# Stick-breaking attention in a hybrid decoder step: page tiles and weight tiles with places of their own

## The chip, the core and the metric

The kernel runs on one NeuronCore of a Trainium2 chip. The metric is the device time of one execution in microseconds (us), as the median of several runs. A profile records one further execution: what each engine did and when. The engines are PE (TensorE, matmuls and transposes), DVE (VectorE), ACT (ScalarE), POOL (GpSimd, which also issues the indirect DMAs) and SP (which issues the other DMAs).

## The reference

One layer of a decoder step for a prompt of 512 tokens behind 16 meta tokens, and for 8 running sequences of 4 new tokens each. All of it is float32.

```python
h = x + 0.5 * rms_norm(swiglu(rms_norm(x, ...), ...), ...)
u = rms_norm(h, mix_pre_g)
proj = u @ w_in          # q, k, v of GLA and of the stick-breaking branch, gates
o_a  = gla_branch(...)   # gated linear attention
o_b  = sb_attend(q_b, keys, vals, sb_bias, q_off)
m = sigmoid(gate_a) * (o_a @ w_o_gla) + sigmoid(gate_b) * (o_b @ w_o_sb)
h = h + rms_norm(m @ w_out, mix_post_g)
y = h + 0.5 * rms_norm(swiglu(rms_norm(h, ...), ...), ...)
```

The change lies in the stick-breaking attention, which has 16 heads of 64. For a query t and the keys s before it:

```python
z = q @ k / sqrt(64) + bias
A[t, s] = sigmoid(z[t, s]) * prod_{s < j < t} (1 - sigmoid(z[t, j]))
o[t] = sum_s A[t, s] * v[s]
```

The prompt attends to itself (528 tokens). Each running sequence attends to 256 cached tokens as well, which lie in 2 pages of 128 tokens of a paged cache (`cache_k`, `cache_v`, found through `page_table`).

## The kernel before

All tokens (512 of the prompt, 32 new ones, 16 meta) lie side by side in the free dimension; features lie in the partitions. A large product is made in three float32r matmuls per tile: `hi` weights with the `hi` and the `lo` part of the activations (L232, L233), `lo` weights with the `hi` part (L235). One **step** of a product is one of its 8 slices of 128 features, for both halves of the tokens: six matmuls. Weights come by DMA into `raw`, ACT copies them to `hi` (L192), DVE subtracts to `lo` (L139, the line of the helper `tt`, which makes all two-operand work).

Almost all other tiles are cut from one arena by `take(width)` and given back by `give(...)`. A tile that is taken again must wait until everything that read or wrote its last tenant is done. Which place is used is decided when the program is built, from the order of the calls.

The stage that is changed is a loop `for pr in range(9)` over 8 pairs of heads; I call one turn of it a **pass**. In pass `pr` PE makes the query, key and value products of pair `now` (24 steps), and between the steps, at places that are written out by hand (`in_q`, `in_k`, `in_v`: after step 1 to 8 of each product), it does the following.

- For the pair before (`last`): `rows_v` and `rows_k` transpose the new rows and write them to DRAM (L895, L884); `rows_v` also splits the values into `hi` and `lo` (`vsp`, the `lo` on POOL); `tails` transposes the last rows and a zero-padded copy of the meta values (`vfm`, filled by two POOL copies, L912). `turned(e, n)` transposes a part of the weights of head `e` (L933) and splits them into `ah` (ACT, L936) and `al` (DVE, L139); `summed(e, n)` multiplies them with the values (L948 to L950, of which the second reads `al`). `meta_turned` and `meta_summed` do the meta part, ending with a copy on ACT (L967).
- For `now`, `scores(e)` after value step 3 (head 0) and 5 (head 1): products on PE (L854, L855) into three banks; two sigmoids of each on ACT (L858, L859) into `keep` and `beta`; 8 triangular selects on POOL (L863); 5 scans on DVE (L867) and three products with `beta` (L139); then four POOL copies of the meta columns into `am` (L876).
- In passes 5 to 8, the samples: `sample_keys` transposes the four gathered pages (16 transposes, L1034, at query steps 1, 3, 5, 7) and `sample_products` multiplies them with the new queries (L1047).

A page is fetched by an indirect DMA on POOL (L992) into a tile from `take(512)`:

```python
if pr > 4:
    kp, kT = pages_of(ck, 0, pr - 5), {}     # four gathers, ahead of the queries
```

PE's order in this loop is fixed by hand. The order on the other engines, and on PE elsewhere, is made by a scheduler when the program is built; on the chip each engine works through its own list in order.

After the loop, `sample_weights` turns the sums of the samples into attention weights (L1070, L1087), and a stage of 8 gate products follows in which `sample_values` (L1154, needs value pages) and `sample_scores` for the second half of the heads (needs key pages) alternate; a stage of 16 products with four more `sample_values` comes next.

Of the kernel before, what the change touches and what calls it, by code (L numbers as in the profile page):

```python
# [9 lines left out]
F32R = mybir.dt.float32r  # L10
# [97 lines left out]
def hybrid_step(  # L108
# [647 lines left out]
        G.memset(t, 0.0)  # L756


    klz = [[take(nk, F32R) for _ in range(2)] for _ in range(2)]
    for t in (*klz[0], *klz[1]):  # L760
        G.memset(t.bitcast(F32), 0.0)

    def qzp(pr, more=128):
# [16 lines left out]
    def steps(main, at):  # L780

        n = 0
        while True:
# [5 lines left out]
            for f in at.get(n, ()):  # L789
                f()  # L790

    class Pair:


        def __init__(self, pr):
            self.pr, self.c0 = pr, P * pr
            self.betas = []

        def queries(self, at):
            pr = self.pr  # L800
# [17 lines left out]
        def keys(self, at):  # L818
            pr = self.pr
            acc = steps(gemm_steps(win, C_KB + self.c0, P, KD, um, (0, 1), HW), at)  # L820

            self.kf = kf = take(NT)
            S.copy(kf[:, NTL : NTL + HW], acc[0][:, :HW])
            S.copy(kf[:, NTL + HW :], acc[1][:, : NP - HW])
            S.copy(kf[:, :NTL], acc[1][:, NP - HW : HW])
            self.ks = ks = [take(nk, F32R) for _ in range(2)]
            self.kl = kl = klz[pr % 2]
            for e in range(2):
                src = kf[own_[e], NS:]
                V.tensor_copy(ks[e][own_[e]], src)  # L830
                S.copy(ks[e][other[e]], src)
                tt(kl[e][own_[e]], src, ks[e][own_[e]].bitcast(F32), ALU.subtract)
            V.tensor_copy(kns[:, NS * pr : NS * pr + NS], kf[:, :NS])

        def values(self, at):
            acc = steps(gemm_steps(win, C_VB + self.c0, P, KD, um, (0, 1), HW), at)
            self.vf = vf = take(NT)
            for h in range(2):
                S.copy(vf[:, h * HW : h * HW + HW], acc[h][:, :HW])

        def scores(self, e):
            hh = 2 * self.pr + e
            qs, ks, kl = self.qs, self.ks, self.kl
            if e == 0:
                self.am = take(P)

            beta, keep = (take(832), take(NP)), (take(832), take(NP))
            for n, what in enumerate(BANKS):
                p = ps()
                c = 0  # L850
                for i, k0, k1 in what:
                    qc, kc = slice(P * i, P * i + P), slice(k0, k1)
                    o = p[:, c : c + k1 - k0]
                    T.matmul(o, qs[e][:, qc], ks[e][:, kc], start=True, stop=False)  # L854
                    T.matmul(o, qs[e][:, qc], kl[e][:, kc], start=False, stop=True)  # L855
                    c += k1 - k0
                d = slice(416 * (n % 2), 416 * (n % 2) + c)
                S.activation(keep[n // 2][:, d], p[:, :c], AF.Sigmoid, bias=sbb[:, 16 + hh : 17 + hh], scale=-1.0)  # L858
                S.activation(beta[n // 2][:, d], p[:, :c], AF.Sigmoid, bias=sbb[:, hh : hh + 1])  # L859
            for i, a, b in PARTS:  # L860
                for t, fill in ((keep, 1.0), (beta, 0.0)):
                    d = t[i // 3][:, b - P : b]
                    G.affine_select(out=d, in_=d, pattern=[[-1, P]], compare_op=ALU.is_ge, fill=fill, base=-1,  # L863
                                    channel_multiplier=1)
            for i, a, b in PARTS + ((2, 816, 832),):
                k = keep[i // 3][:, a:b][:, ::-1]
                V.tensor_tensor_scan(out=k, data0=k, data1=k, initial=keep[1][:, :1] if a == 816 else 1.0,  # L867
                                     op0=ALU.mult, op1=ALU.bypass)
            for d, k in ((beta[0][:, :831], keep[0][:, 1:832]), (beta[0][:, 831:832], keep[1][:, :1]),
                         (beta[1][:, : NP - 1], keep[1][:, 1:])):  # L870
                tt(d, d, k, ALU.mult)
            give(*keep)
            self.betas.append(beta)
            for i in range(4):
                a = (0, 144, 416, 816)[i]
                G.tensor_copy(self.am[:, 2 * NM * i + NM * e : 2 * NM * i + NM * e + NM], beta[0][:, a : a + NM])  # L876
            if e:
                give(*qs, *ks)

# [26 lines left out]

        def tails(self):
            pr, kf, vf = self.pr, self.kf, self.vf
            vz = vfm[pr % 2]
            for e in range(2):  # L910
                o = vz[own_[e]].rearrange("p (i e k) -> p i e k", e=2, k=NM)[:, :, e]
                G.tensor_copy(o, vf[own_[e], NP + NS :].unsqueeze(1).to_broadcast([64, 4, NM]))  # L912
            p = ps()
            T.transpose(p[:NTL, :P], kf[:, :NTL], ident)
            T.transpose(p[:NTL, P : 2 * P], vf[:, NP:], ident)
            T.transpose(p[:, 2 * P : 3 * P], vz, ident)
            fc = slice(P * (pr % 4), P * (pr % 4) + P)
            self.vm = vm = take(P)
            V.tensor_copy(tail_k[pr // 4][:NTL, fc], p[:NTL, :P])
            V.tensor_copy(tail_v[pr // 4][:NTL, fc], p[:NTL, P : 2 * P])  # L920
            V.tensor_copy(vm, p[:, 2 * P : 3 * P])
            give(kf, vf)
# [17 lines left out]
        def summed(self, e, n):  # L940

            where, ah, al = self.at.pop((e, n))
            if (e, n) == (0, 0):
                self.op = ps()
            for j, c in where:
                o, w = self.op[:, P * j :], P * (4 - j)
                vh, vl = (t[:, P * j : P * j + P] for t in vsp[e])
                T.matmul(o, vh, ah[:, c : c + w], start=(j == 0 and e == 0), stop=False)  # L948
                T.matmul(o, vh, al[:, c : c + w], start=False, stop=False)  # L949
                T.matmul(o, vl, ah[:, c : c + w], start=False, stop=False)  # L950
            give(ah, al)
            if n == len(TILES) - 1:
                give(*self.betas[e])

        at = property(lambda self: self.__dict__.setdefault("at_", {}))

# [30 lines left out]
    ck = cache_k.rearrange("o n s (c h) d -> (o n s c) (h d)", c=2)  # L987
    cv = cache_v.rearrange("o n s (c h) d -> (o n s c) (h d)", c=2)

    def page(src, i, c):  # L990
        t = take(512)
        G.indirect_dma_start(out=t, out_offset=None, in_=src,  # L992
                             in_offset=bass.IndirectOffsetOnAxis(ap=idx[c][:, i : i + 1].bitcast(U32), axis=0))
        return t
# [30 lines left out]
    def pages_of(src, c, b0):  # L1025
        return {(b, pg): page(src, 2 * b + pg, c) for b in (b0, b0 + 4) for pg in range(2)}

    def sample_keys(b, q, kp, kT):

        p = ps()  # L1030
        for r in range(2):
            f = slice(P * (2 * q + r), P * (2 * q + r) + P)
            for pg in range(2):
                T.transpose(p[:, 256 * r + P * pg : 256 * r + P * pg + P], kp[b, pg][:, f], ident)  # L1034
        kT[b, q] = take(512)
        (S.copy if q else V.tensor_copy)(kT[b, q], p)
        if q:
            give(kp[b, 0], kp[b, 1])

    def sample_products(c, b0, kT, z):  # L1040

# [60 lines left out]

    z = take(512)
    with tc.manual_schedule(engines={mybir.EngineType.PE}):
        last = None
        for pr in range(9):
            now = Pair(pr) if pr < 8 else None
            in_q, in_k, in_v = {}, {}, {}
            if last:
# [8 lines left out]
                in_v[4] = [lambda: last.turned(1, 2), lambda: last.summed(1, 1)]  # L1118
                in_v[6] = [lambda: last.summed(1, 2), last.meta_summed]
            if pr > 4:  # L1120
                kp, kT = pages_of(ck, 0, pr - 5), {}
                for n, (b, q) in enumerate((b, q) for b in (pr - 5, pr - 1) for q in range(2)):
                    in_q.setdefault(2 * n + 1, []).append(lambda b=b, q=q: sample_keys(b, q, kp, kT))
                in_k[1] = [lambda: sample_products(0, pr - 5, kT, z)]
            if now:
                in_v.setdefault(3, []).append(lambda: now.scores(0))
                in_v.setdefault(5, []).append(lambda: now.scores(1))
                now.queries(in_q)
                now.keys(in_k)
                now.values(in_v)  # L1130
            else:
# [2 lines left out]
                        for f in at[n]:  # L1134
                            f()
            last = now
    give(*vfm, *klz[0], *klz[1], *vsp[0], *vsp[1], mmask)
    sample_weights(0, z)
    give(z)
    for c in range(2):  # L1140
# [6 lines left out]
    def sample_values(c, b0, vp, oz):  # L1147

        for pg in range(2):
            for i in range(4):  # L1150
                q, r = 2 * c + i // 2, i % 2
                for b in (b0, b0 + 4):
                    row = slice(64 * r + 32 * (b // 4), 64 * r + 32 * (b // 4) + 32)
                    T.matmul(oz[row, P * q : P * q + P], aT[q, pg][:, 256 * r + 32 * b : 256 * r + 32 * b + 32],  # L1154
                             vp[b, pg][:, P * i : P * i + P], start=False, stop=(b0 == 3 and c == 1 and pg == 1 and i > 1))
        give(*vp.values())
        if b0 == 3:
            give(*(aT[g, pg] for g in (2 * c, 2 * c + 1) for pg in range(2)))

# [22 lines left out]

    oas, oap = Parts(), []
    z, oz = take(512), ps()
    vp = pages_of(cv, 0, 0)
    kp = pages_of(ck, 1, 0)
    sample_new(0, oz)
# [22 lines left out]
    for n in range(8):  # L1210
        if n % 2 == 0:
            sample_values(1, n // 2, vp, oz)
            vp = pages_of(cv, 1, n // 2 + 1) if n < 6 else {}
        acc = mgemm(C_GA + P * n, P, W1)
        sg = take(NW)
        for h in range(2):
# [97 lines left out]
```

## Time and profile before

| | us |
|---|---|
| median of 3 runs | 1711.05 (1708.38 to 1714.02) |
| profiled execution | 1711.21 |
| its span, first to last instruction | 1709.5 |
| PE busy | 1615.0 (94%) |
| DVE busy | 805.1 (47%) |
| ACT busy | 637.3 (37%) |
| POOL busy | 340.4 (20%) |
| mean granted clock of PE | 0.982 |

The page gives the busy time of each engine over the whole span. A windows view gives, for stretches that one chooses, the length, the busy time of PE, of its weight loads (PEld), of DVE, ACT and POOL with the number of instructions, the granted clock of PE, the DMAs' busy share and GB/s. A view of waits gives the waiting engine with its line, what ended the wait, the total in us, how often, and the longest. A timeline gives start, duration, engine, line and operation, and in brackets the idle time of the engine just before and what ended it. Line numbers are those of the kernel before.

### The profile page before, as it was taken

The page shows a single profiled execution, that of the slowest core. Times are in us where ns is not written, and L with a number is a line of the kernel's source. Part 1 is how long each engine was busy: PE and PEld are TensorE (multiplying, and loading weights), DVE is VectorE, ACT ScalarE, POOL GpSimd, SP SyncE. Part 2 cuts the span into 40 slices and gives each one's busy share as a digit, 9 for nine tenths or more (in the row PEclk, how much of TensorE's full clock was granted, in tenths as well). Part 3 has the DMA queues.
Part 4 walks back from the last instruction along what each step waited for, and adds up shares of the span by engine and source line. Part 5 has one row for each costly group of instructions (what it writes and reads, how often), then busy time and mean ns, then how long its engine had stood idle before and what let it go on. Part 6 is the DMA issues. An engine that isn't in the chain of part 4 may idle for free.

```text
span 1709.5 us, 29997 instructions
## 1 busy us (share of the span) xinstructions
PE 1615.0 (94%) x12473; PEld 1548.1 (91%) x12473; DVE 805.1 (47%) x1371; ACT 637.3 (37%) x1094; POOL 340.4 (20%) x480
## 2 busy tenths in 40 slices
PE   7999999999798999998787999999999999999997
PEld 6999999999687788888776798999999999999997
DVE  5533333326545676776554543243545333332246
ACT  6422222224334345565443332233346322222233
POOL 2111111100110124244333762010301111110001
PEclk9999999999899999999998999999999999999998
DMA  6422222234666444424333566344403323233243
GB/s 167 136 87 87 87 87 83 80 91 136 142 121 131 124 94 76 78 57 92 78 63 71 174 168 184 82 76 128 136 26 99 112 87 87 87 87 90 83 128 114
DMA packets 296776, 176.02 MB, mean 103 GB/s; under 512 B 9002, under 2 KB 288640, under 8 KB 296640
## 3 DMA queue, kind: packets, MB, share of 16 engines
q1 hardware_dynamic: 291200, 157.25, 37.1%
q0 software_dynamic: 5440, 16.85, 2.8%
q8 instruction: 98, 1.61, 0.4%
q14 instruction: 38, 0.31, 0.1%
HBM read 160.25 MB, written 13.83 MB: 102 GB/s over the span
## 4 chain that ended last, share of the span: by engine, by line
PE 54%; DVE 6%; DMA 6%; issue 5%; ACT 2%; POOL 1%; SPq 0%; ACTq 0%; POOLq 0%; DVEq 0%
PE acc L232 15%; PE acc L233 15%; PE acc L235 15%; DMA raw<-in_w_in_dram 4%; DVE room L139 2%; DVE room L142 1%; DVE lo L139 1%; DMA room<-in_cache_k_dram,idx 1%; ACT hi L192 1%; PE ps L1034 1%; DMA out_dram<-room 1%; DVE room L867 1%; PE ps L949 1%; PE ps L933 1%; POOL room L863 1%
## 5 line engine op out<-in xcount | busy, mean ns | idle before, releaser
L232 PE MATMUL acc<-room,hi 128*128 128x280 f32 (+2 forms) x3440 | 969.3, 295 | 4.2 <-ACT hi L192 3.5
L233 PE MATMUL acc<-room,hi 128*128 128x280 f32 (+2 forms) x3440 | 952.9, 292 | 0.0
L235 PE MATMUL acc<-room,lo 128*128 128x280 f32 (+2 forms) x3440 | 774.9, 292 | 3.0 <-DVE lo L139 2.9
L232 PEld LDWEIGHTS acc<-room,hi 128*128 128x128 f32 (+1 forms) x3440 | 651.6, 189 | 17.0 <-issue 7.5
L233 PEld LDWEIGHTS acc<-room,hi 128*128 128x128 f32 (+1 forms) x3440 | 651.8, 190 | 8.5 <-issue 5.8
L235 PEld LDWEIGHTS acc<-room,lo 128*128 128x128 f32 (+1 forms) x3440 | 562.0, 189 | 6.7 <-DVE lo L139 4.1
L192 ACT CAST hi<-raw 128x1024 fp32r<-128x1024 f32 (+1 forms) x258 | 264.5, 1025 | 743.3 <-PE acc L233 639.7
L139 DVE TENSOR_TENSOR lo<-raw,hi 128x1024 fp32r<-128x1024 f32 (+1 forms) x258 | 312.6, 1212 | 306.8 <-ACT hi L192 300.3
L139 POOL TENSOR_TENSOR room<-room,room 128x544 fp32r<-128x544 f32 (+6 forms) x118 | 148.7, 1270 | 988.5 <-ACT room L394 471.7
L139 DVE TENSOR_TENSOR room<-acc,room 128x280 f32<-128x280 f32 (+1 forms) x262 | 106.6, 440 | 395.0 <-PE acc L235 394.4
L139 DVE TENSOR_TENSOR room<-room,room 128x280 f32<-128x280 f32 (+10 forms) x173 | 98.1, 583 | 31.5 <-ACT room L260 24.9
L863 POOL TENSOR_SCALAR_AFFINE_SELECT room<-room 128x128 f32<-128x128 f32 x128 | 56.1, 463 | 96.5 <-ACT room L858 93.4
L867 DVE TENSOR_TENSOR_SCAN room<-room 128x144 f32<-128x144 f32 (+4 forms) x71 | 58.4, 846 | 17.5 <-POOL room L863 16.1
L139 DVE TENSOR_TENSOR room<-ps,room 128x384 fp32r<-128x384 f32 (+3 forms) x64 | 35.9, 577 | 20.0 <-ACT room L936 19.5
L992 POOL DMA_INDIRECT room<-in_cache_v_dram,idx x32 | 35.7, 1114 | 32.7 <-DMA out_dram<-room 8.4
L992 POOL DMA_INDIRECT room<-in_cache_k_dram,idx x32 | 33.1, 1034 | 42.0 <-PE ps L959 16.1
L854 PE MATMUL ps<-room,room 128*128 128x144 f32 (+4 forms) x75 | 23.2, 327 | 16.9 <-DVE room L139 14.5
L858 ACT ACTIVATE room<-ps,sbb 128x416 f32<-128x416 f32 (+1 forms) x48 | 30.5, 640 | 21.6 <-PE ps L855 18.4
L936 ACT CAST room<-ps 128x384 fp32r<-128x384 f32 (+1 forms) x48 | 24.5, 515 | 28.6 <-PE ps L933 28.5
L260 ACT ACTIVATE room<-room 128x280 f32<-128x280 f32 (+1 forms) x56 | 24.1, 432 | 29.0 <-DVE room L139 22.6
L1034 PE MATMUL ps<-ident,room 128*128 128x128 f32 x128 | 18.9, 283 | 15.1 <-DMA room<-in_cache_k_dram,idx 15.1
L394 ACT CAST room<-room 128x560 fp32r<-128x560 f32 (+1 forms) x44 | 28.8, 655 | 11.6 <-DVE room L139 9.9
(302 smaller groups left out, 1249.7 us busy)
## 6 DMA issues: line engine op xcount, KB each, us to landing
raw<-in_w_in_dram SPq DMA_DIRECT2D x72, 512.0 KB, 8.8
raw<-in_ffn_w_gate_dram SPq DMA_DIRECT2D x50, 512.0 KB, 3.8
raw<-in_ffn_w_up_dram SPq DMA_DIRECT2D x50, 512.0 KB, 3.9
raw<-in_ffn_w_down_dram SPq DMA_DIRECT2D x44, 448.0 KB, 3.7
raw<-in_ffn_w_down_dram SPq DMA_DIRECT2D x22, 512.0 KB, 3.9
out_dram<-room SPq DMA_DIRECT2D x40, 256.0 KB, 3.4
room<-in_state_gla_dram SPq DMA_DIRECT2D x16, 256.0 KB, 3.8
raw<-in_w_o_gla_dram SPq DMA_DIRECT2D x8, 512.0 KB, 4.5
```

Source lines behind the costliest of these rows:

```text
L139: (eng or V).tensor_tensor(out=out, in0=a, in1=b, op=op)
L192: S.copy(hi, raw)
L232: T.matmul(o, wh, a[h][0], start=(k == 0), stop=False)
L233: T.matmul(o, wh, a[h][1], start=False, stop=False)
L235: T.matmul(acc[h][:nw, : wid[h]], wl, a[h][0], start=False, stop=(k == kt - 1))
L394: S.copy(hi[:, c], sl[:, c])
L858: S.activation(keep[n // 2][:, d], p[:, :c], AF.Sigmoid, bias=sbb[:, 16 + hh : 17 + hh], scale=-1.0)
L863: G.affine_select(out=d, in_=d, pattern=[[-1, P]], compare_op=ALU.is_ge, fill=fill, base=-1, channel_multiplier=1)
L867: V.tensor_tensor_scan(out=k, data0=k, data1=k, initial=keep[1][:, :1] if a == 816 else 1.0, op0=ALU.mult, op1=ALU.bypass)
L936: S.copy(ah[:, :c], p[:, :c])
L992: G.indirect_dma_start(out=t, out_offset=None, in_=src, in_offset=bass.IndirectOffsetOnAxis(ap=idx[c][:, i : i + 1].bitcast(U32), axis=0))
L1034: T.transpose(p[:, 256 * r + P * pg : 256 * r + P * pg + P], kp[b, pg][:, f], ident)
```

## The change

It has these parts.

1. `wide`: four sets of tiles (832 and 512 wide) are taken once for `beta` and `keep` and used in turn, in place of `take` and `give` in every call of `scores`. The sets of both `keep` come back at the end of `scores(1)`, those of `beta` when `summed` of the next pass has read them. For that, `scores(1)` moves from value step 5 to 6, behind `summed(1, 2)` and `meta_summed`.
2. `ring`: page tiles are taken once (four from pass 4, four more after the loop) and used in turn. The gathers for the next pass are written down after the queries of this one, from pass 4 on. After the loop, key and value pages share the ring of eight.
3. The four `am` copies of a head move from POOL to DVE. The two `vfm` copies move to DVE as well, and from `tails` to the end of `values`, one pass part earlier.
4. `klz`, the zero-padded `lo` parts of the keys, is one set in place of two in turn.

```diff
-    klz = [[take(nk, F32R) for _ in range(2)] for _ in range(2)]
-    for t in (*klz[0], *klz[1]):
+    klz = [take(nk, F32R) for _ in range(2)]
+    for t in klz:
...
+    wide = [(take(832), take(NP)) for _ in range(4)]
...
-            self.kl = kl = klz[pr % 2]
+            self.kl = kl = klz
...
         def values(self, at):
...
+            vz = vfm[self.pr % 2]
+            for e in range(2):
+                o = vz[own_[e]].rearrange("p (i e k) -> p i e k", e=2, k=NM)[:, :, e]
+                V.tensor_copy(o, vf[own_[e], NP + NS :].unsqueeze(1).to_broadcast([64, 4, NM]))
...
-            beta, keep = (take(832), take(NP)), (take(832), take(NP))
+            beta, keep = wide.pop(0), wide.pop(0)
...
-            give(*keep)
+            self.keeps.append(keep)
+            if e:
+                wide.extend(self.keeps)
             self.betas.append(beta)
             for i in range(4):
                 a = (0, 144, 416, 816)[i]
-                G.tensor_copy(self.am[...], beta[0][:, a : a + NM])
+                V.tensor_copy(self.am[...], beta[0][:, a : a + NM])
...
         def tails(self):
-            vz = vfm[pr % 2]
-            for e in range(2):
-                o = vz[own_[e]].rearrange("p (i e k) -> p i e k", e=2, k=NM)[:, :, e]
-                G.tensor_copy(o, vf[own_[e], NP + NS :].unsqueeze(1).to_broadcast([64, 4, NM]))
...
             if n == len(TILES) - 1:
-                give(*self.betas[e])
+                wide.append(self.betas[e])
...
+    ring = []
+
     def page(src, i, c):
-        t = take(512)
+        t = ring.pop(0)
...
         if q:
-            give(kp[b, 0], kp[b, 1])
+            ring.extend((kp[b, 0], kp[b, 1]))
...
-        last = None
+        last = kp_next = None
         for pr in range(9):
+            kp = kp_next
+            if pr == 4:
+                ring += [take(512) for _ in range(4)]
...
             if pr > 4:
-                kp, kT = pages_of(ck, 0, pr - 5), {}
+                kT = {}
...
                 in_v.setdefault(3, []).append(lambda: now.scores(0))
-                in_v.setdefault(5, []).append(lambda: now.scores(1))
+                in_v.setdefault(6, []).append(lambda: now.scores(1))
                 now.queries(in_q)
+                if pr > 3:
+                    kp_next = pages_of(ck, 0, pr - 4)
                 now.keys(in_k)
                 now.values(in_v)
...
-        give(*vp.values())
+        ring.extend(vp.values())
...
+    ring += [take(512) for _ in range(4)]
     vp = pages_of(cv, 0, 0)
     kp = pages_of(ck, 1, 0)
...
-            vp = pages_of(cv, 1, n // 2 + 1) if n < 6 else {}
+            vp = pages_of(cv, 1, n // 2 + 1) if n < 6 else give(*ring)
```

More of the change, by code (lines that the diff above doesn't have):

```diff
@@ L796, in __init__ @@
             self.pr, self.c0 = pr, P * pr
-            self.betas = []
+            self.betas, self.keeps = [], []
         def queries(self, at):
@@ L875, in scores @@
                 a = (0, 144, 416, 816)[i]
-                G.tensor_copy(self.am[:, 2 * NM * i + NM * e : 2 * NM * i + NM * e + NM], beta[0][:, a : a + NM])
+                V.tensor_copy(self.am[:, 2 * NM * i + NM * e : 2 * NM * i + NM * e + NM], beta[0][:, a : a + NM])
             if e:
@@ L915, in tails @@
             T.transpose(p[:NTL, P : 2 * P], vf[:, NP:], ident)
-            T.transpose(p[:, 2 * P : 3 * P], vz, ident)
+            T.transpose(p[:, 2 * P : 3 * P], vfm[pr % 2], ident)
             fc = slice(P * (pr % 4), P * (pr % 4) + P)
@@ L1136, in hybrid_step @@
             last = now
-    give(*vfm, *klz[0], *klz[1], *vsp[0], *vsp[1], mmask)
+    give(*vfm, *klz, *vsp[0], *vsp[1], mmask)
+    for t in wide:
+        give(*t)
     sample_weights(0, z)
```

## The prediction

> **What bounds the kernel now.** First the page: what is busy over the whole span, then the windows cut at the copies of `meta_summed` (ACT L967), which end the last step of each pair, so that one window is one pass of the pair loop.
>
> ```profile
> span 1709.5 us, 29997 instructions
> PE 1615.0 (94%) x12473; PEld 1548.1 (91%) x12473; DVE 805.1 (47%) x1371; ACT 637.3 (37%) x1094; POOL 340.4 (20%) x480
> ...
> 703.80:735.40 31.60, 30.29 (x224) 28.77 (x223) 23.28 (x43) 18.73 (x37) 11.47 (x29) 1.00 0.31 68
> 735.40:767.10 31.70, 30.41 (x224) 28.91 (x224) 23.38 (x43) 18.66 (x38) 11.54 (x29) 1.00 0.29 67
> 767.10:803.90 36.80, 31.61 (x224) 30.21 (x223) 27.04 (x48) 18.92 (x37) 18.47 (x36) 0.95 0.44 99
> 803.90:842.80 38.90, 33.96 (x256) 31.12 (x255) 22.00 (x42) 19.92 (x39) 10.13 (x25) 1.00 0.28 62
> 842.80:887.50 44.70, 36.68 (x255) 33.59 (x255) 27.07 (x47) 19.80 (x39) 16.48 (x37) 0.89 0.31 71
> 887.50:940.20 52.70, 38.69 (x269) 35.70 (x268) 25.10 (x46) 19.95 (x39) 19.22 (x36) 0.90 0.32 72
> ```
>
> PE is the bound, at 94%, so only its idle time and its clock can be won. The first two windows (passes 2 and 3) are what a pass costs when nothing holds it: 31.65 us. The last four (passes 4 to 7) take 36.8, 38.9, 44.7 and 52.7 us, with the granted clock down to 0.89 in two of them. Passes 5 to 7 do more work (the page transposes and the sample products): PE's busy time rises from 30.35 to 33.96 us in the one of them with a full clock, so 3.6 us. The rest is waiting. Next who is waited for there, by PE and by POOL, between 780 and 960 us, and POOL's timeline:
>
> ```profile
> PE ps L1034 <- DMA room<-in_cache_k_dram,idx: 15.1, 3, 7.5
> PE ps L854 <- DVE room L139: 13.4, 8, 4.5
> ...
> POOL room L992 <- PE ps L959: 16.1, 1, 16.1
> POOL room L912 <- DMA room<-in_cache_k_dram,idx: 13.7, 2, 12.1
> POOL room L992 <- PE ps L950: 13.6, 1, 13.6
> ...
> 783.25 1.12 POOL L992 DMA_INDIRECT room<-in_cache_v_dram,idx  x1 [8.37 <-DMA out_dram<-room]
> 787.40 0.96 POOL L992 DMA_INDIRECT room<-in_cache_k_dram,idx  x1 [3.03 <-PE ps L933]
> ...
> 792.14 2.62 POOL L863 TENSOR_SCALAR_AFFINE_SELECT room<-room 128x128 f32<-128x128 f32 x8
> ```
>
> PE waits 15.1 us for pages that land late, and 13.4 us at the score products (L854) for DVE. The second is the same cause at one remove: gathers (L992) stand in POOL's list before the selects (L863) and wait for a place in the arena, here until a write to DRAM and PE's transposes have let go of it. Selects, scans (L867) and everything on DVE behind them come late.
>
> **The gathers and the fixed tiles.** The changed program hands POOL the same 16 key gathers of the first half in groups of four that stand among the two `lo` subtractions of `rows_v`, each waiting for PE's reads of the four tiles of its ring; the selects come after them (one gather of the first group, two passes early, is the exception). The tiles are read within the query product of one pass and used next in that of the following, over 20 us later, against a landing that I quote below. So both waits of PE above go. Behind a waiting gather on POOL stand the second `lo` subtraction, wanted only by `summed(1, 0)` late in the key/value products, and selects that come later still: no one waits for that. SP is moved past nothing. Worth: passes 4 to 7 took 36.8 + 38.9 + 44.7 + 52.7 = 173.1 us and should take 31.65 + 3 x (31.65 + 3.6) = 137.4 us. Gain 35.7 us (bounds 33, if passes 5 to 7 keep 0.9 us of other waits each, and 37, if the 3.6 is 0.4 too much). Their lost clock is in these windows, so it isn't counted again.
>
> **The scores of the second head, moved from value step 5 to 6.** This is the price that the change adds, since the second `beta` of the last pair must be read first. The timeline of a clean pass:
>
> ```profile
> 725.44 0.23 PE L854 MATMUL ps<-room 128*128 128x144 f32 x1
> ...
> 727.83 0.29 PE L232 MATMUL acc<-room,hi 128*128 128x280 f32 x1
> ...
> 728.61 0.49 PE L933 MATMUL ps<-ident,room 128*128 128x128 f32 x3
> ...
> 730.24 0.23 PE L854 MATMUL ps<-room,room 128*128 128x144 f32 x1
> ...
> 731.40 1.76 DVE L139 TENSOR_TENSOR room<-room,room 128x1 f32<-128x1 f32 x3
> ...
> 732.07 0.50 PE L854 MATMUL ps<-room,room 128*128 128x512 f32 x1 [0.71 <-ACT room L859]
> ...
> 733.09 0.55 DVE L139 TENSOR_TENSOR room<-ps,room 128x384 fp32r<-128x384 f32 x1
> 733.41 0.28 PE L948 MATMUL ps<-room,room 128*128 128x256 f32 x1
> ```
>
> Scores of head 0 begin at 725.44. One step (six matmuls) takes 728.61 - 727.83 = 0.78 us. `turned(1, 2)` follows at 728.61; its `al` half is made on DVE at 733.09 to 733.64, because in DVE's list it stands behind head 0's scans and products (the three at 731.40), before and after the change alike. PE reads `al` in `summed(1, 2)` at 733.41: just in time, because the scores of head 1 (730.24 on, with a wait of 0.71 us for a bank) lie between. Moved behind `summed`, they no longer do. PE then reaches `summed(1, 2)` at 730.24 + 0.78 = 731.0, does one matmul of 0.1 us, and waits until 733.64: a gap of 2.5 us. The 0.71 us goes, since the banks have long been drained then. Net 1.8 us a pass. Passes 1 to 6 have it; in pass 7 the changed order of PE has 2.5 steps of the next product in that place. 6 x 1.8 = 10.8 us (bounds 6 and 15). Queued behind the wait on PE are `meta_summed`, head 1's scores and two steps; the reader of those scores, `turned(1, 0)`, stands 2 + 8 + 8 steps on.
>
> Such gaps touch the clock. PE's busy time in stretches of 3.41 us, and the granted clock (the number before the DMA share):
>
> ```profile
> 881.30:884.71 3.41, 1.54 (x10) 1.46 (x11) 2.76 (x5) 1.94 (x4) 1.87 (x8) 1.00 0.02 6
> 884.71:888.12 3.41, 3.41 (x12) 2.38 (x11) 2.88 (x6) 1.90 (x4) 2.38 (x6) 0.50 0.01 2
> ...
> 949.57:952.98 3.41, 1.60 (x12) 1.24 (x10) 0.00 (x0) 0.71 (x2) 1.21 (x2) 1.00 0.91 308
> 952.98:956.40 3.42, 2.82 (x20) 2.56 (x20) 1.66 (x4) 1.51 (x4) 2.36 (x3) 1.00 0.28 102
> ```
>
> After a stretch with 1.54 us busy the clock is halved for the next 3.41 us; after one with 1.60 it is not. So a gap costs a half window, 3.41/2 = 1.7 us, when more than about 1.83 us of it falls into one stretch. For a gap of 2.5 us that holds for starts in 2.25 of 3.41 us: 4 times in 6, so 4 x 1.7 = 6.8 us (bounds 0 and 10.2). The Trainium skill, "TensorE: Matmul & The Clock Gate", section on HAM oscillation, gives the rule that only idle gaps above about 3.4 us bring the clock down. By it this term would be zero and the time 6.8 us less. The stretch at 881.30 speaks against it, with an idle time of 1.87 us; I keep the term and take the rule as a rival.
>
> **The copies on VectorE.** The eight `am` copies and two `vfm` copies of a pass leave POOL and join DVE:
>
> ```profile
> L876 POOL COPY room<-room x64: 186/193/1515, 674.5 to 943.1; 128x16 f32<-128x16 f32 x64
> ...
> L833 DVE COPY room<-room x8: 181/181/197, 666.8 to 925.9; 128x32 f32<-128x32 f32 x8
> ...
> 739.57 1.22 DVE L139 TENSOR_TENSOR lo<-raw,hi 128x1024 fp32r<-128x1024 f32 x1
> ...
> 744.51 0.42 PE L235 MATMUL acc<-room,lo 128*128 128x280 f32 x2
> ```
>
> The nearest DVE row is the 128x32 copy, 0.18 us: 10 x 0.18 = 1.8 us a pass on an engine that is busy 23.3 of 31.6. In the list the `am` copies of head 0 stand behind `al`, so they don't lengthen the gap above. Those of head 1 stand ahead of the `lo` of the key weights, which ended at 740.79 and was first read at 744.51: cover 3.7 us. It shrinks, because head 1's chain now starts 4.7 us later (at 733.64 plus some 1.3 us for the rest of `summed` and `meta_summed`, in place of 730.24) on a PE that is 1.8 us later (2.9 us less cover) with 0.9 us of copies in it and 1.2 us of `al` out of the way. About 1 us is left, so nothing in passes 1 to 3. In passes 5 to 7 two page copies come on top, and I take 0.5 us each: 1.5 us (bounds 0 and 7, 1 us in each of seven passes). Leaving POOL saves its 0.19 us a copy and gains nothing, POOL being idle two thirds of a pass. One key zero set less (`klz`) changes no wait: its writer runs 16 steps after the last reader.
>
> **The start of the next stage.** Products and values of the samples now share a ring of eight tiles:
>
> ```profile
> 957.18 0.95 POOL L992 DMA_INDIRECT room<-in_cache_v_dram,idx  x1 [0.30 <-issue]
> ...
> 959.74 0.54 PE L1070 MATMUL ps<-room,room 128*32 128x32 f32 x26
> ...
> 964.07 0.41 PE L1087 MATMUL ps<-ident,room 128*128 128x128 f32 x2 [0.27 <-DVE room L139]
> ...
> DMA to landing us min/median/max: 3.3/5.2/14.9
> ```
>
> In the changed order of PE the last transposes of `sample_weights` come 2.5 steps (1.9 us) after its products, where they were ready 964.07 - 960.28 = 3.8 us after: 1.9 us of wait, and about 1 us more for the copies of the weights behind them. The second set of values is asked for only when the first has been read, and is used after 8 steps (6.2 us) and a page of transposes and products (some 3 us): four gathers 1.25 us apart and a landing of 5.2 us make 10.2 us, so 1 us late, or 10.7 by the landing of 14.9. Later sets have 16 steps. I take 5 us in all (bounds 0 and 14). From 1060 us on the order of every engine is the same but for names of rooms: nothing.
>
> **Sum**, against the profiled execution (1711.2 us, its span of 1709.5 and 1.7 around it; the median of the runs, 1711.05, is the same): -35.7 + 10.8 + 6.8 + 1.5 + 5 = -11.6, so 1699.6, say 1700 us.
>
> **Rivals.**
> The clock holds: the gaps of 2.5 us stay without a halved window, and the start of the next stage is covered as it was. For it: gaps of this size at full clock exist (949.57). 1699.6 - 6.8 - 5 = 1688 us.
> DVE becomes the late one: the cover of 1 us above is gone, and PE waits for `lo` or for a bank in each of seven passes, 2 us each. For it, DVE would be busy 25 of 33 us in a strict list; against it, the cover as I count it. 1699.6 + 14 - 1.5 = 1712 us.
> The change does less than it says: one gather of the first group stands in the middle of a set of selects two passes early, and may hang there as the one at 783.25 did; one late chain of some 5 us and a halved window give 1706 us.
> Slower: the ring paces the next stage. A set is asked for only after the set before it in its tiles has been read, and is wanted 16 steps later, 12.3 us plus transposes and products, some 17 us. With the longest landing it needs 5 + 14.9 = 19.9 us. It decides from a landing of 12 us on; then nine sets are 2.9 us late, with a half window of 1.7: 41 us, 1741 us. Against it: a median of 5.2.
>
> **Chances.** Forecast 0.45, clock holds 0.22, DVE late 0.20, less than it says 0.05, ring 0.08. A measurement of this kernel tells 0.3%, 5.1 us, from no change. Faster: 0.38 of the forecast's 0.45, all of 0.22, 0.03 of DVE, 0.02: 0.65. Slower: 0.08 and 0.04 of the two before: 0.12. The rest, 0.23, is the same. The bounds of the terms together run from 1680 (-37 + 6 + 0 + 0 + 0 = -31) to 1724 (-33 + 15 + 10.2 + 7 + 14 = +13). That all of them fall on one side is less likely than 2 in 10 with the ring's 0.08 beside it, so I take off 4 us below and 8 above: 1684 to 1716, which holds the forecast and the three rivals before the ring.
>
> **What would show it.** Right: passes 4 to 7 at 33 to 38 us each; no wait of L1041 (then the page transposes) for a gather; a wait of about 2.5 us on `al` (DVE L139) at the first `al` product of `summed`, six times, and a clock of 0.5 behind some. Wrong: gathers still waiting between selects, or PE waiting for `lo`, or for gathers after 960 us at each set; or no gap at `summed` at all, which would leave 1682.

## The result and the profile after

| | before | after |
|---|---|---|
| median of 4 runs, us | 1711.76 (1708.38 to 1714.02) | 1740.11 (1737.33 to 1742.16) |
| ratio, 95% interval | 1 | 1.0166 [1.0143, 1.0189] |
| profiled execution, us | 1711.21 | 1740.88 |
| mean granted clock of PE | 0.982 | 0.972 |

The change makes the kernel 1.7% slower, where 0.7% faster was forecast. First the page after, and the windows of its passes 2 to 8, cut as before at the copies of `meta_summed`, which now are line L972. From here on, the lines in a view are those of the kernel that it shows.

```profile
span 1739.2 us, 29944 instructions
PE 1622.9 (93%) x12473; PEld 1552.4 (89%) x12473; DVE 820.1 (47%) x1451; ACT 635.6 (37%) x1094; POOL 313.4 (18%) x398
```

```profile
709.30:744.40 35.10, 31.92 (x224) 29.67 (x223) 25.37 (x52) 18.46 (x38) 8.56 (x18) 0.95 0.26 61
744.40:781.60 37.20, 31.83 (x224) 29.60 (x224) 25.89 (x52) 18.47 (x37) 13.57 (x22) 0.96 0.33 86
781.60:815.50 33.90, 30.78 (x225) 29.07 (x224) 25.38 (x52) 18.52 (x38) 8.56 (x18) 0.99 0.35 68
815.50:864.20 48.70, 36.45 (x256) 32.90 (x255) 27.37 (x55) 19.52 (x39) 13.39 (x22) 0.89 0.27 66
864.20:905.10 40.90, 36.65 (x256) 33.32 (x255) 27.08 (x55) 19.73 (x39) 13.67 (x22) 0.92 0.32 78
905.10:956.80 51.70, 38.88 (x273) 35.69 (x271) 27.22 (x55) 19.82 (x39) 14.08 (x24) 0.87 0.25 61
956.80:989.20 32.40, 26.59 (x220) 22.06 (x221) 16.77 (x29) 13.58 (x27) 13.09 (x19) 0.95 0.41 109
```

PE does the same 12473 matmuls. Pass 2 begins at 709.3, in the kernel before at 703.8: 5.5 us are lost by then. Passes 4 to 7 take 33.9 + 48.7 + 40.9 + 51.7 = 175.2 us against 173.1 before: the gain of 35.7 us that was to come here is not there. The last pass ends at 989.2, in the kernel before 29.4 us earlier, at 959.8; the spans differ by 29.7. So in sum nothing is won or lost behind the loop. The 29.4 us are 5.5 ahead of pass 2, 9.0 in passes 2 and 3 (72.3 us against 63.3), 2.1 in passes 4 to 7 and 12.8 in pass 8 (32.4 us against 19.6, with 60 more matmuls in it).

Who waits, in the list of PE's waits over the whole span (waiting line, what ended the wait, total us, times, longest):

```profile
PE ps L954 <- DVE room L139: 15.8, 9, 2.5
PE ps L1054 <- DVE room L1043: 15.3, 3, 8.9
...
PE ps L1054 <- ACT room L1043: 11.8, 1, 11.8
PE ps L720 <- DVE room L723: 7.5, 1, 7.5
...
PE ps L921 <- DVE room L846: 4.1, 5, 2.2
```

No wait for a gathered page is left among them: that part of the change works. The first row is the gap at the `al` products that was forecast. The next three were not. L1054 is `sample_products`; it waits for L1043, the copies of the transposed keys into `kT`, on DVE and on ACT. L720 stands in the gated branch just ahead of the loop. What those copies wait for is in DVE's, ACT's and SP's timeline:

```profile
662.58 0.48 DVE L1016 COPY room<-sbb 1x256 f32<-1x256 f32 x2 [8.14 <-DMA out_dram<-room]
662.99 0.23 DVE L723 TENSOR_SCALAR room<-ps,gains 128x32 f32<-128x32 f32 x1
663.15 0.34 DVE L819 TENSOR_SCALAR room<-acc 64x16 f32<-64x16 f32 x2
663.27 0.17 PEld L720 LDWEIGHTS ps<-ident,room 32*128 32x128 f32 x1 [7.71 <-DVE room L723]
...
826.99 0.53 SPq L896 DMA_DIRECT2D out_dram<-room  x1
...
837.42 0.69 DVE L1043 COPY room<-ps 128x512 f32<-128x512 f32 x1 [10.32 <-DMA out_dram<-room]
...
916.90 0.58 SPq L896 DMA_DIRECT2D out_dram<-room  x1
...
931.64 0.59 ACT L1043 COPY room<-ps 128x512 f32<-128x512 f32 x1 [12.04 <-DMA out_dram<-room]
```

In all three the engine stands still for 8 to 12 us until a write from the arena to DRAM (`out_dram<-room`) is done. L896 is the write of the new key rows in `rows_k`. It is issued at 826.99, and the copy into `kT` starts at 837.42, some 10 us later: `kT` was given the place that the rows are still being read from. A third such wait, of 4.1 us on DVE, stands in pass 8. The waits of DVE and ACT for these writes, over the whole span:

```profile
DVE room L1043 <- DMA out_dram<-room: 14.4, 2, 10.3
...
ACT room L1043 <- DMA out_dram<-room: 12.0, 1, 12.0
```

The order of `take` and `give` in the two programs says the same. `take` prefers, among the free places that fit without waste, the one given back longest ago. In the changed kernel so few are free that the third `kT` of pass 5, the fourth of pass 7 and the third of pass 8 get the place of `kt`, the tile of the new key rows, which was given back just before; these are the three copies that wait. (The kernel before too gives `kT` places of the new rows, in passes 5 and 6. ACT waits for writes at its copies there, 7.3 us in all and at most 5.2 at once; PE also waits for late pages in these passes.)

L1016 fills `bt`, a tile with the bias of the samples, the first operation of the attention stage; it stands in DVE's list ahead of L723, and L723 ahead of PE's L720. Its place is one of a state tile (`s0`) that the gated branch is still writing out; in the kernel before it is one given back longer ago.

After these waits the clock is low for longer than after the small ones:

```profile
829.99:833.40 3.41, 0.00 (x0) 0.00 (x0) 0.00 (x0) 0.00 (x0) 0.00 (x0) 0.99 0.79 112
833.40:843.60 10.20, 5.44 (x29) 4.16 (x30) 4.85 (x12) 1.25 (x3) 0.00 (x0) 0.50 0.47 143
843.60:847.00 3.40, 3.40 (x26) 3.27 (x26) 0.95 (x2) 0.48 (x1) 0.00 (x0) 1.00 0.08 22
```

PE is idle from 829.2 to 838.2. The clock is halved from 833.4 on, while PE is still idle, and comes back at 843.6: 10.2 us. So one wait of 9 us costs 9 us and about half of the 5.4 us that PE works at half rate behind it. Stretches of the same length belong to the gaps at L720 (from 659.3) and at 920.5 (from 925.5); PE works 6.2 and 3.5 us in them.

### The profile page after: what moved, and what is told of

Same layout as the page of the kernel before. It is cut to its first block, busy times and chain, and to the rows that moved or that the text cites. A ratio compares the mean times of both kernels' runs of the same rounds, so it can differ in the third digit from the quotient of the medians.

```text
span 1739.2 us, 29944 instructions
## 1 busy us (share of the span) xinstructions
PE 1622.9 (93%) x12473; PEld 1552.4 (89%) x12473; DVE 820.1 (47%) x1451; ACT 635.6 (37%) x1094; POOL 313.4 (18%) x398
## 4 chain that ended last, share of the span: by engine, by line
PE 47%; issue 12%; DVE 6%; DMA 6%; POOL 3%; ACT 1%; another core or an unknown queue 1%; SPq 0%; POOLq 0%; ACTq 0%; DVEq 0%
PE acc L232 13%; PE acc L233 13%; PE acc L235 13%; DMA raw<-in_w_in_dram 4%; DVE room L139 2%; POOL room L870 2%; DMA out_dram<-room 2%; DVE lo L139 1%; DVE room L874 1%; DVE room L142 1%; ACT hi L192 1%; PE ps L1054 0%; PE ps L449 0%; POOL room L139 0%
## 5 line engine op out<-in xcount | busy, mean ns | idle before, releaser
L235 PE MATMUL acc<-room,lo 128*128 128x280 f32 (+2 forms) x3440 | 775.2, 292 | 1.9 <-DVE lo L139 1.9
L235 PEld LDWEIGHTS acc<-room,lo 128*128 128x128 f32 (+1 forms) x3440 | 562.5, 189 | 5.3 <-DVE lo L139 2.6
L139 POOL TENSOR_TENSOR room<-room,room 128x544 fp32r<-128x544 f32 (+6 forms) x118 | 154.1, 1315 | 974.5 <-ACT room L394 468.7
L139 DVE TENSOR_TENSOR room<-room,room 128x280 f32<-128x280 f32 (+10 forms) x174 | 102.0, 606 | 31.4 <-ACT room L260 24.9
L870 POOL TENSOR_SCALAR_AFFINE_SELECT room<-room 128x128 f32<-128x128 f32 x128 | 51.5, 428 | 175.8 <-ACT room L865 135.3
L874 DVE TENSOR_TENSOR_SCAN room<-room 128x144 f32<-128x144 f32 (+4 forms) x72 | 58.6, 831 | 36.5 <-POOL room L870 34.4
L1054 PE MATMUL ps<-room,room 128*32 128x256 f32 x128 | 15.9, 480 | 27.1 <-DVE room L1043 15.3
L999 POOL DMA_INDIRECT room<-in_cache_v_dram,idx x32 | 33.5, 1046 | 35.7 <-PE ps L1168 26.5
L954 PE MATMUL ps<-room,room 128*128 128x512 f32 (+3 forms) x62 | 22.0, 355 | 15.8 <-DVE room L139 15.8
L865 ACT ACTIVATE room<-ps,sbb 128x416 f32<-128x416 f32 (+1 forms) x48 | 30.7, 640 | 13.8 <-PE ps L862 13.7
L1054 PEld LDWEIGHTS ps<-room,room 128*32 128x32 f32 x128 | 4.8, 126 | 32.7 <-DVE room L1043 16.5
```

The lines of the kernel that those rows point to most:

```text
L139: (eng or V).tensor_tensor(out=out, in0=a, in1=b, op=op)
L235: T.matmul(acc[h][:nw, : wid[h]], wl, a[h][0], start=False, stop=(k == kt - 1))
L999: G.indirect_dma_start(out=t, out_offset=None, in_=src, in_offset=bass.IndirectOffsetOnAxis(ap=idx[c][:, i : i + 1].bitcast(U32), axis=0))
```

## The experiments

**Theory W**: the tiles held throughout (four `wide` sets, the ring) leave the arena so few free places that `kT` and `bt` get one left a short time ago by a tile that is being written to DRAM. **Rivals**: the gap at `al` with its halved clock, where `scores(1)` was moved, is the loss; or the copies are, on a DVE that works through a strict list; or the ring itself is. Beside them stands the prediction, by its own terms. The first four kernels start from the kernel after. The first leaves the writes out; the next three have them and take the suspected costs away, one more in each.

### The row writes left out

```diff
-            nc.sync.dma_start(kp_out[...], kt...)     # rows_k
-            nc.sync.dma_start(vp_out[...], vt...)     # rows_v
```

> The changed kernel without the two writes of new key and value rows to DRAM in rows_k and rows_v (16 DMAs of 256 KB; those outputs are left out). The places of all tiles stay as they are. Theory W (the tiles kT of the transposed pages are cut from places whose last tenant is still being written to DRAM): the gaps of PE at sample_products of 8.95, 11.75 and 4.04 us and the halved windows behind them (10.24, 10.24 and 3.41 us at half rate, so 12 us) go; 36.7 us at most, some of it met by the next wait: 1703 to 1715 us. Rival D (DVE is late there because of its ten added copies a pass): the copies on DVE stand where they stood, the gaps stay, 1735 to 1742 us. Rival G (the gathered pages land late): the gaps stay as well.

This kernel leaves the rows of new keys and values in DRAM unwritten. Measured: 1704.88 us (1699.81 to 1711.97), ratio to the kernel before 0.9991 [0.997, 1.0013]; 35.2 us below the kernel after. (The two were measured at different times, and the kernel before took 1711.76 us beside the one and 1708.09 beside the other; by the ratios it is 1.75%, some 30 us.) Passes 4 to 7:

```profile
778.00:811.90 33.90, 30.91 (x225) 29.22 (x224) 25.37 (x52) 18.48 (x37) 8.54 (x18) 0.99 0.29 53
811.90:850.70 38.80, 35.12 (x256) 31.92 (x256) 27.37 (x55) 19.49 (x40) 14.34 (x22) 0.96 0.29 69
850.70:887.80 37.10, 33.63 (x256) 30.99 (x256) 27.29 (x55) 19.54 (x39) 14.05 (x22) 1.00 0.31 72
887.80:925.00 37.20, 35.52 (x273) 32.88 (x271) 27.21 (x55) 19.47 (x39) 14.46 (x24) 1.00 0.31 71
```

They take 147.0 us in place of 175.2, the clock is at 0.96 to 1.00, and the long waits at the sample products are gone from PE's list; a late DVE or late pages would have left them. What is left there:

```profile
PE ps L950 <- DVE room L139: 16.8, 12, 2.5
...
PE ps L720 <- DVE room L723: 7.4, 1, 7.4
```

W holds for the passes. The `al` gaps (here L950) are still there, so they are not what the forecast lacked; it had priced them. The gap of 7.4 us ahead of the loop stays, as its write is another one.

### A place of its own for kT

`kT` is put into the `keep` tiles of the pair before, whose last reader is long done by then.

```diff
-        kT[b, q] = take(512)
+        kT[b, q] = place        # last.keeps[n // 2]: [1], or [0][:, :512]
...
-        give(*kT.values())
```

> The changed kernel with the four kT tiles of a pass in the keep tiles of the pair before, which lie idle from the end of scores(1) to the next scores(0); nothing else. Theory W: the three gaps at sample_products go, because no write to DRAM ever holds a keep tile: 1703 to 1715 us, as without the writes. The gap of 7.5 us at the transposes of GLA's last head (place of bt, also behind a write) stays. Rival D or G: 1735 to 1742 us.

Measured: 1704.27 us (1697.7 to 1710.16), 0.9974 [0.9955, 0.9994]. With all writes in place this gives what leaving them out gave. So the writes cost nothing by themselves that these runs could tell; the place behind them does. The row of L720 stays:

```profile
PE ps L954 <- DVE room L139: 16.7, 11, 2.5
...
PE ps L720 <- DVE room L723: 7.5, 1, 7.5
```

### A place for bt as well

```diff
-    bt = take(512)
+    bt = wide[3][1]         # idle until scores(1) of pass 0
```

> As the one before, and the row bt of biases in a keep tile too. Theory W: the gap of 7.5 us and its 10.24 us at half rate, 12.6 us, go as well: 1690 to 1702 us, faster than the kernel before; what is left over it is the gap of 2.5 us at summed(1, 2) in passes 1 to 6. Rival: the gap at GLA's last head comes from the order of PE there, and stays: as the one before.

Measured: 1692.82 us (1690.97 to 1695.98), 0.9907 [0.9872, 0.9941]. The row of L720 is gone from PE's list, whose first rows in the attention stage are now:

```profile
PE ps L954 <- DVE room L139: 16.5, 11, 2.5
...
PE ps L921 <- DVE room L846: 4.6, 5, 2.2
```

The step from the kernel without this place is 11.5 us, for a wait of 7.5 us and 6.2 us of work at half clock. With both places apart the change gains 15.3 us on the kernel before, measured beside it (1708.09); forecast were 11.6.

### The transposes of the second head earlier

The price of moving `scores(1)` is the wait for `al`. Here `turned(1, 2)`, which makes `al`, goes ahead of head 0's scores.

```diff
-    in_v[4] = [lambda: last.turned(1, 2), lambda: last.summed(1, 1)]
+    in_v[3] = [lambda: last.turned(1, 2)]
+    in_v[4] = [lambda: last.summed(1, 1)]
```

> As the one before, and turned(1, 2) moved from value step 4 to step 3, ahead of scores(0), so that its al part stands ahead of the scans of head 0 in the list of DVE. By the prediction's step the six gaps of 2.5 us at summed(1, 2) and four halved windows, 6 x 1.8 + 4 x 1.7 = 17.6 us, go: 1673 to 1686 us. Rival: DVE's whole list is late at that place, the gap moves to the next product of summed or to the scores, and less than 6 us is won.

Measured: 1675.29 us (1670.87 to 1677.53), 0.9809 [0.9777, 0.9841]: 17.5 us below the last one.

```profile
PE ps L861 <- DVE room L139: 6.1, 7, 1.7
...
PE ps L921 <- DVE room L846: 4.6, 5, 1.9
...
PE ps L954 <- DVE room L139: 1.9, 4, 0.6
```

The six gaps at L954 are gone (16.5 to 1.9 us in all), and with them the halved window behind one. So the rival is right about the price, and 10.8 and 6.8 us had been forecast for it, 17.6 in all: it is a part of the slowdown, but not the part that the forecast lacked. That the sum agrees so well is luck in part: in the profiled execution of the kernel without the move one of the six gaps is followed by a halved window, where four were forecast, so most of the 17.5 us are the gaps themselves, and 1.8 us of wait come back at L861 (4.3 to 6.1). What is left is L921, a transpose of `vfm` that waits for the copies which the change moved to DVE. In DVE's timeline they stand behind products that wait for scans:

```profile
735.18 3.41 DVE L139 TENSOR_TENSOR room<-room,room 128x1 f32<-128x1 f32 x3
...
738.51 0.38 DVE L846 COPY room<-room 64x64 f32<-64x64 f32 x2
...
738.95 0.33 PE L921 MATMUL ps<-ident,room 128*128 128x128 f32 x1 [1.89 <-DVE room L846]
```

### The parts alone

The other way round, one part at a time was put into the kernel before. First the ring with the early gathers and the single `klz`:

```diff
-    t = take(512)                          # page()
+    t = ring.pop(0)
...
+    if pr > 3:
+        kp_next = pages_of(ck, 0, pr - 4)  # behind the queries
```

> The kernel before with the ring of page tiles and its early gathers, and with one set of klz (without which the ring doesn't fit); scores, copies and their tiles as before. By the prediction's first step taken alone: the waits for pages go, -35.7 us, 1672 to 1680 us. By theory W: the waits of L1034 for gathers go too, but kT copies and sigmoids still take places that are being written to DRAM, with gaps of 5 to 12 us in some of passes 5 to 8 and halved windows behind them, so that 10 to 35 us are given back: 1685 to 1715 us.

Measured: 1705.96 us (1704.53 to 1708.82), 0.9975 [0.9962, 0.9988]. This is what W expected; of the 35.7 us that the prediction's first step would give alone, 4 to 5 are there. The waits for gathered pages are gone, and others have come:

```profile
PE ps L854 <- DVE room L139: 16.2, 13, 2.3
...
PE ps L1049 <- ACT room L886: 7.5, 1, 7.5
```

The second is W again with another tile. ACT's copy into the tile of the key rows (L886) stands still behind a write, and with it the `kT` copy next in ACT's list:

```profile
904.27 0.58 ACT L886 COPY room<-ps 128x512 f32<-128x512 f32 x1 [12.37 <-DMA out_dram<-room]
904.75 0.59 ACT L1038 COPY room<-ps 128x512 f32<-128x512 f32 x1
```

The first is a gap of 2.2 us in five passes, at the scores of the second head: their sigmoid waits until DVE's products of the first head are done. By the order of `take` and `give` it is a place again: in passes 2 to 6 one of the second head's tiles gets the place of the first head's `keep`, which these products still read; in the kernel before this is so only in passes 4 and 6 of the five. No run of its own tests it.

Then the `wide` sets with `scores(1)` at step 6:

```diff
+    wide = [(take(832), take(NP)) for _ in range(4)]
...
-    in_v.setdefault(5, []).append(lambda: now.scores(1))
+    in_v.setdefault(6, []).append(lambda: now.scores(1))
```

> The kernel before with the four fixed sets for beta and keep alone, and scores(1) at value step 6 for it; gathers, copies and klz as before. By the prediction: six gaps of 2.5 us at summed(1, 2) with four halved windows, +17.6 us, and the gathers' waits of passes 4 to 7 unchanged: 1725 to 1733 us. By theory W: in addition the row bt takes a place behind a write, +12.6 us, and kT as well: 1735 to 1765 us.

Measured: 1723.48 us (1716.29 to 1725.54), 1.0058 [1.0036, 1.0081].

```profile
PE ps L953 <- DVE room L139: 18.0, 12, 4.0
...
PE ps L720 <- DVE room L723: 7.6, 1, 7.6
```

It has the price at `al` and the stall of `bt`, so the second belongs to the `wide` sets and not to the ring (in the run of the ring alone L720 does not wait). It undercut both expectations, since part of the gather waits went without a ring: pass 7 takes 40.6 us in place of 52.7. That was not foreseen, and no run tells why.

And the copies on DVE:

```diff
-    G.tensor_copy(...)      # am, vfm
+    V.tensor_copy(...)
```

> The kernel before with the am and vfm copies on DVE alone. By the prediction: nothing in passes 1 to 3, up to 1.5 us in passes 5 to 7: 1708 to 1714 us. Rival: the copies stood on POOL between selects and gathers, where POOL waits 20 us for DVE before them; without them gathers and selects start earlier, 1695 to 1707 us. Other rival: the vfm copies make tails wait, as a gap of 2.2 us does once in the changed kernel, and cost 3 to 6 us.

Measured: 1712.02 us (1706.75 to 1715.87), 1.0001 [0.9984, 1.0017]. Nothing: neither rival shows, and put into the kernel before, the copies cost nothing. The ring alone loses nothing either. The parts alone come to -0.25%, +0.6% and 0, which is +0.3%; together they are +1.7%. The rest lies between the parts, and I put it down to `wide` and the ring, which draw on one arena. Alone, each shows one long wait of PE behind a write (7.5 and 7.6 us); together there are the one at `bt` and two of 9 and 12 us at `kT`.

### The version without any of these waits

The fourth kernel with the two `vfm` copies back on POOL and in `tails`.

```diff
-                V.tensor_copy(o, vf...)    # values
+                G.tensor_copy(o, vf...)    # tails
```

> The best version so far (kT and bt in keep tiles, turned(1, 2) ahead of scores(0)), with the two vfm copies back in tails on POOL; the am copies stay on DVE. If the waits of the third transpose of tails for DVE (4.6 us in five places) are the price of that move: 2 to 5 us less, 1670 to 1674 us. Rival: POOL's vfm copies then stand behind the selects and PE waits as long: 1674 to 1679 us.

Measured: 1664.58 us (1661.26 to 1666.2), 0.9719 [0.9693, 0.9745]: 2.8% below the kernel before, and the fastest here. Passes 4 to 7:

```profile
756.80:787.50 30.70, 30.00 (x224) 28.69 (x223) 25.43 (x51) 18.37 (x37) 11.11 (x21) 1.00 0.40 85
787.50:822.00 34.50, 33.36 (x258) 31.02 (x256) 26.06 (x54) 19.50 (x40) 14.36 (x24) 1.00 0.36 93
822.00:856.40 34.40, 33.24 (x256) 30.92 (x255) 25.89 (x54) 19.47 (x39) 14.41 (x24) 1.00 0.39 93
856.40:893.90 37.50, 34.96 (x258) 32.58 (x257) 27.16 (x55) 19.61 (x39) 15.73 (x26) 0.95 0.35 85
```

Their sum is 137.1 us. The gain was more than expected: 10.7 us between the medians (15 by the two ratios, 0.9809 and 0.9719), for waits at L921 of 4.6 us in all. The two profiled executions differ by 4.7 us (1670.87 and 1666.2), about that wait; the rest I can't name. So the `vfm` copies on DVE cost something here, though nothing in the kernel before; why they differ, no run shows.

## Why the prediction was wrong

**The step that failed** is the first term, "The gathers and the fixed tiles": "both waits of PE above go", worth -35.7 us, with bounds of 33 and 37. The waits went. But the term took the passes to be free of all waits, because it asked only what the new tiles release and never what they take. Tiles that are held throughout are no longer places for others: `kT` and `bt`, which the change doesn't touch, were handed places behind writes to DRAM. In the kernel after this costs 8.95 + 11.75 + 4.04 us of PE's time at the sample products (the last in pass 8) and 7.48 us at L720, and behind these gaps PE works some 18 us at half clock. Priced by kernels that differ only in these places, it is 1740.11 - 1704.27 = 35.8 us for `kT` (33 by the ratios, as the two were measured at different times) and 1704.27 - 1692.82 = 11.5 us for `bt`, 44 to 47 us together. The forecast missed by 40.1.

It could have been seen. Which place a tile gets is fixed when the program is built, and the changed kernel was there to be read: which tile had `kT`'s place before it, and what reads it last. The prediction looks at the order of the instructions on each engine, and in that order nothing is wrong; the wait lies in an operand.

**The size of that term was right** once the places are apart: forecast were 137.4 us for passes 4 to 7, and the last kernel, without the gaps at `al` too, takes 137.1. That it is so close is luck in part: 30.7, 34.5 and 34.4 us are each somewhat less than the 31.65 and 35.25 of the sum, and 37.5 is more.

**The scores of the second head: right.** Six gaps at the first `al` product of `summed(1, 2)` were forecast, of 2.5 us each; they are 2.35, 2.37, 2.40, 2.35, 2.53 and 2.34 us. "In DVE's list it stands behind head 0's scans and products" holds: in the fourth of them DVE works on the three products until 813.25 and on `al` until 813.71, and PE goes on at 813.76.

**The clock: right in kind, and in the count by luck.** Four of the six gaps were to be followed by a halved window, and four are. The same six gaps stand in the profiles of the first three experiments, and there it is three, two and one; so the 6.8 us were too much on the average. Stretches of 3.41 us on the grid of the clock, two and two:

```profile
703.65:707.06 3.41, 1.57 (x13) 1.36 (x11) 3.26 (x7) 0.43 (x2) 0.45 (x2) 1.00 0.12 31
707.06:710.48 3.42, 2.91 (x17) 2.39 (x18) 0.77 (x5) 1.18 (x3) 0.02 (x1) 1.00 0.00 0
737.78:741.20 3.42, 1.05 (x10) 0.84 (x8) 3.38 (x9) 0.00 (x0) 0.00 (x0) 1.00 0.00 0
741.20:744.61 3.41, 3.41 (x10) 2.38 (x11) 0.24 (x4) 0.25 (x1) 0.00 (x0) 0.50 0.00 0
```

With 1.05 us busy the next stretch is halved, with 1.57 it is not. At another of the six gaps a stretch with 1.60 us is followed by a halved one (from 860.66), so in this run the limit lies near 1.6 us and is no sharp line. The Trainium skill, "TensorE: Matmul & The Clock Gate", section on HAM oscillation, puts the rule as "no PE-idle gaps >~3.4µs". This trace does not agree that shorter gaps are free: the one of 2.37 us at 738.81 was followed by a halved stretch. The rival in which the clock holds falls with it; the term stands, with a smaller size.

**The copies on VectorE: a cost, but in another place.** 1.5 us was forecast, for a cover of `lo` that gets thin; PE's wait for `lo` at L235 is 1.9 us in the whole span, where it was 2.9 before, so that cost did not come, nor the rival of a late DVE with its 2 us a pass. What I did not price is the two `vfm` copies: taken along with the `am` copies as ten copies of 0.18 us, they have a reader on PE a few steps on. In the kernel after PE waits 4.1 us for them, and more is won when they go back.

**The start of the next stage: too dear.** 5 us were forecast; before and after differ by 29.4 us at 960 and 989 us and by 29.7 at the end, so in sum 0.3. The wait at the last transposes of `sample_weights` is 1.0 us in place of 1.9 (L1094, at 992 and 993), and no wait for a value page stands in the list. It is a sum with parts that were not foreseen: PE waits 4.5 us at L1094 for the second half of the heads (at 1064) and 2.3 us for a `kT` (at 1001), so as much must be gained elsewhere. **After 1060 us nothing: right.** The rival that ended at 1741 us, a ring that paces the next stage, names the time and not the mechanism: the loss is made before that stage begins.

## What to carry to other kernels

A tile that is held for good is paid for by all others that share its memory. When tiles are given places of their own, list every tile that has to move because of it, and for each who used its new place last; a place whose last reader is a DMA to DRAM came free 7 to 15 us after its issue here, and an engine that waits for it holds back its whole list. Write outs should have places that nothing urgent is given next, and the order of instructions alone will not show it.

## What was not expected of the hardware

A write of 128 x 512 float32 from the arena lets go of its source only some 10 us after its issue: 10.4 us (826.99 to 837.42), 14.7 (916.90 to 931.64) and 7.4 (968.8 to 976.22, in pass 8). And the clock is half for 10.2 us, three stretches of 3.41 us, at gaps of 7 to 12 us, where after gaps of 2.3 to 2.5 us it was half for 3.41 or, once, for 6.8. The first part of the 10.2 us lies in the gap itself. In this trace the clock came back after a halved stretch in which PE was busy for 3.17 us or more (from 976.72; 3.41 from 741.20), and stayed half after 2.03 us (from 836.77) and 3.08 us (from 901.62).
